# A one-core transformer block: two modulation rows change place, a reciprocal and a set of attention masks move ahead in DVE's order

## The chip, the core and the metric

The kernel runs on one core of a Trainium2 chip. A core has a matrix engine (PE), a vector engine (DVE), an activation engine (ACT), a general engine (POOL) and a queue engine (SP) that here only issues DMA transfers. Each engine runs its own instructions in the order in which they were written and waits on semaphores where an operand, or room for a result, comes from elsewhere. PE writes its products into banks of a small accumulation memory; DVE and ACT read them from there. The metric is the device time of one execution in microseconds (us).

## The reference

One decoder block on 512 tokens of width 1024, all in f32. A conditioning vector gives nine modulation vectors of 1024 (a shift, a scale and a gate for each of three sub-layers):

```
mod = silu(c) @ w_ada + b_ada
sh1, sc1, gt1, sh2, sc2, gt2, sh3, sc3, gt3 = split(mod, 9)
u = rmsnorm(h, g1) * (1 + sc1) + sh1;  h = h + 0.5 * gt1 * swiglu(u, w_ffn1_in, w_ffn1_out)
u = rmsnorm(h, g2) * (1 + sc2) + sh2;  h = h + gt2 * token_mixing(u)
u = rmsnorm(h, g3) * (1 + sc3) + sh3;  h = h + 0.5 * gt3 * swiglu(u, w_ffn2_in, w_ffn2_out)
return rmsnorm(h, g_final)
```

`swiglu` is `(silu(a) * b) @ w_out` with `a, b = split(u @ w_in)` and 2816 hidden columns. `token_mixing` projects u once, runs a causal pooling mixer and a causal dilated window attention in three head groups with rotary q and k, merges them with sigmoid gates and projects back.

## The kernel before

Activations lie with features on the 128 partitions and tokens along the row: H is eight tiles of 128 x 512. A product in f32 precision is made of three matmuls: a value is split into a high part and a rest, and `mm3` adds high times high, high times rest and rest times high. Weights come from memory in chunks of 128 x 1024 (or 768), issued by SP (L295, named after their source: `wf1i`, `wf1o`, `wmix`, `wf2i`, `wf2o`) into a few buffers, `raw` and parts of `X`. For each chunk ACT writes the high part `whi` (L377) and DVE the rest `wlo` (L389) into a ring that PE reads. A buffer is loaded again when its `wlo` has been written. Large products of the feed-forwards and the gates are made from seven block products instead of eight, with sums of blocks made by DVE (`duo`, `out_blocks`).

The order on each engine is the order in which the program calls its helpers; there is no planner. Work that is not tied to a place is put in by hand.

Such work are the modulation rows. Each of the 72 rows is 128 values of `mod`: SP loads a 128 x 1024 piece of `w_ada` (L440), and DVE multiplies it with the conditioning and sums along the row (`ada_do`, L448). `bg()` does the next row and then starts the load of a later one into a free buffer; `ada_stop` says up to which row. After every eighth row two small operations finish the vector (L459, L461). Rows 24 to 39 belong to gate, shift and scale around the first feed-forward's end, and are done within its hidden pairs: `ROWS` says after which of a pair's seven block products a row stands. Rows from 40 on are done in the mixer.

The first feed-forward's output comes in five parts over the hidden columns. The last part (columns 16 to 21, `ffn` at its end and `out_tail`) goes tile by tile. Tiles 0 to 3 are done whole: PE makes the product, DVE adds it to H (L1272), ACT squares H, DVE adds the square to AR, which collects the sum for the next norm (L499). Tiles 4 to 7 are done in two halves of 256 tokens: first half of all four, then second half of all four (L582, L583, L623). While PE is at the second halves, the first half's norm is finished: PE sums AR over the partitions (`stats_t`, L509), ACT takes the root, DVE the reciprocal `r` (L514), PE spreads it (`spread`, L519), and `norm_steps` makes the normalised halves, per tile one scaled `ev` (L533), the high part UH by ACT (L545) and the rest UL by DVE (L559).

`head` then starts the next sub-layer, the mixer or the second feed-forward, with four weight chunks at once. It runs the first half's eight feature tiles, puts the second half's statistics in after four steps, spreads them after eight, and goes on with the second half. Its ACT table changes there, from the root to what the sub-layer needs.

In the mixer's first stretch, v of the first head group is projected in four token blocks (the loop with `rope_b`), then q and k of the other groups tile by tile with attention steps hooked in at the sixth of eight feature steps: scores on PE, masks and row maxima on DVE (`at_exp`, L1472), exponentials on ACT, and one tile later the transposes on PE (`at_turn`, L1489).

## Time and profile before

| what | value |
|---|---|
| median of three executions | 970.0 us (968.23 to 970.03) |
| the profiled execution | 969.99 us, span 968.2 us |
| PE busy | 958.5 us, 99% of the span |
| DVE busy | 840.3 us, 87% |
| ACT busy | 539.3 us, 56% |
| POOL busy | 89.8 us, 9% |
| DMA issues of modulation rows on SP | 512 KB each, landing after 3.5 to 8.8 us, median 5.1 |

The span is what the profile covers; the execution's own time is 1.8 us more. A row of a timeline has the start, the busy time, the engine, the line and the operation with its output and inputs; in brackets stands how long the engine was idle before it and what ended that. Busy times of neighbours overlap a little, those of matmuls by more than half, so the time that one costs is the distance between two starts. A DVE operation on 128 x 1024 values takes 1.2 us of busy time, a matmul on 256 tokens follows the last after 0.11, one on 512 after 0.23.

### The profile page before, as it was taken

To read this page: it belongs to the slowest core of one execution; us is meant where nothing else is said; L and a number is where in the kernel's file an instruction comes from. 1 tells how busy PE (TensorE), PEld (TensorE's weight loads), DVE (VectorE), ACT (ScalarE), POOL (GpSimd) and SP (SyncE) were. 2 spreads that over 40 slices of the span, in tenths; PEclk is the share of its full clock that TensorE was granted. 3 is DMA by queue.
4 is the path that set the end of the run, shared out by engine and by line. 5 is a ranking of instruction groups with operands and counts; after the bars stand their busy time and mean duration, and the time that the engine had idled before them with its cause. 6 is when DMAs were issued, how large, how long until landed. Compare 5 with 4: busy or idle time off the path is not lost.

```text
span 968.2 us, 18169 instructions
## 1 busy us (share of the span) xinstructions
PE 958.5 (99%) x7296; PEld 899.9 (93%) x7296; DVE 840.3 (87%) x1237; ACT 539.3 (56%) x813; POOL 89.8 (9%) x106
## 2 busy tenths in 40 slices
PE   9999999999999999999999999999999999999997
PEld 7888999999999899778889998998999999999997
DVE  7989999899998778787897877989799888989886
ACT  5443666665755553444565453365666747566655
POOL 0000110101010003005510000000101000110002
PEclk9999999999999999999999999999999999999999
DMA  9857785776768648766457445723757666665632
GB/s 353 283 178 257 197 239 156 202 212 153 219 176 246 171 148 238 239 206 188 90 141 199 124 126 207 243 73 104 194 141 198 170 157 167 172 171 143 169 83 88
DMA packets 54087, 174.71 MB, mean 180 GB/s; under 512 B 7793, under 2 KB 10481, under 8 KB 53746
## 3 DMA queue, kind: packets, MB, share of 16 engines
q1 hardware_dynamic: 44416, 141.29, 44.2%
q0 software_dynamic: 9008, 31.72, 18.1%
q8 instruction: 57, 0.93, 0.4%
q10 hardware_dynamic: 578, 0.53, 0.2%
q14 instruction: 28, 0.23, 0.1%
HBM read 135.36 MB, written 2.24 MB: 142 GB/s over the span
## 4 chain that ended last, share of the span: by engine, by line
PE 84%; DVE 7%; DMA 4%; issue 2%; ACT 1%; POOL 0%; SPq 0%; POOLq 0%; DVEq 0%; ACTq 0%
PE bank L750 13%; PE bank L749 12%; PE bank L751 12%; PE bank L421 7%; PE bank L422 7%; PE bank L423 7%; PE bank L1109 4%; PE bank L1108 4%; PE bank L1110 4%; DVE wlo L389 2%; PE bank L2119 2%; PE bank L2121 1%; PE bank L2123 1%; DMA v<-wada 1%; DMA cs<-wada 1%
## 5 line engine op out<-in xcount | busy, mean ns | idle before, releaser
L389 DVE TENSOR_TENSOR wlo<-raw,whi 128x1024 fp32r<-128x1024 f32 (+3 forms) x150 | 166.4, 1118 | 37.7 <-ACT whi L377 37.5
L749 PE MATMUL bank<-UH,whi 128*128 128x256 f32 x672 | 185.7, 276 | 0.0
L750 PE MATMUL bank<-UL,whi 128*128 128x256 f32 x672 | 185.6, 276 | 0.0
L751 PE MATMUL bank<-UH,wlo 128*128 128x256 f32 x672 | 185.6, 276 | 0.0
L389 DVE TENSOR_TENSOR wlo<-X,whi 128x1024 fp32r<-128x1024 f32 (+3 forms) x133 | 142.2, 1082 | 17.8 <-ACT whi L377 17.6
L377 ACT ACTIVATE whi<-raw 128x1024 fp32r<-128x1024 f32 (+3 forms) x150 | 142.6, 964 | 22.1 <-DMA raw<-wf1o 8.4
L377 ACT ACTIVATE whi<-X 128x1024 fp32r<-128x1024 f32 (+3 forms) x133 | 123.0, 946 | 51.0 <-DVE X L312 46.1
L750 PEld LDWEIGHTS bank<-UL,whi 128*128 128x128 f32 x672 | 126.3, 188 | 0.0
L749 PEld LDWEIGHTS bank<-UH,whi 128*128 128x128 f32 x672 | 126.1, 188 | 0.2
L751 PEld LDWEIGHTS bank<-UH,wlo 128*128 128x128 f32 x672 | 126.2, 188 | 0.0
L751 PE MATMUL bank<-SH,wlo 128*128 128x256 f32 x408 | 112.7, 276 | 0.2 <-DVE wlo L389 0.2
L749 PE MATMUL bank<-SH,whi 128*128 128x256 f32 x408 | 112.6, 276 | 0.0
L750 PE MATMUL bank<-SL,whi 128*128 128x256 f32 x408 | 112.6, 276 | 0.0
L421 PE MATMUL bank<-UH,whi 128*128 128x512 f32 (+1 forms) x272 | 93.0, 342 | 0.0
L422 PE MATMUL bank<-UL,whi 128*128 128x512 f32 (+1 forms) x272 | 92.0, 338 | 0.0
L423 PE MATMUL bank<-UH,wlo 128*128 128x512 f32 (+1 forms) x272 | 91.8, 337 | 0.0
L751 PEld LDWEIGHTS bank<-SH,wlo 128*128 128x128 f32 x408 | 76.6, 188 | 0.4 <-DVE wlo L389 0.4
L749 PEld LDWEIGHTS bank<-SH,whi 128*128 128x128 f32 x408 | 76.6, 188 | 0.0
L750 PEld LDWEIGHTS bank<-SL,whi 128*128 128x128 f32 x408 | 76.6, 188 | 0.0
L1108 PE MATMUL bank<-HI,whi 128*128 128x256 f32 x224 | 61.8, 276 | 0.0
L1109 PE MATMUL bank<-HK,whi 128*128 128x256 f32 x224 | 61.8, 276 | 0.0
L1110 PE MATMUL bank<-HI,wlo 128*128 128x256 f32 x224 | 61.8, 276 | 0.0
(406 smaller groups left out, 2410.9 us busy)
## 6 DMA issues: line engine op xcount, KB each, us to landing
raw<-wmix SPq DMA_DIRECT2D x44, 512.0 KB, 4.3
raw<-wf1i SPq DMA_DIRECT2D x32, 512.0 KB, 5.9
raw<-wf2i SPq DMA_DIRECT2D x30, 512.0 KB, 4.3
ada<-wada SPq DMA_DIRECT2D x23, 512.0 KB, 5.2
X<-raw POOLq DMA_DIRECT2D x23, 512.0 KB, 6.0
xs<-wada SPq DMA_DIRECT2D x17, 512.0 KB, 5.3
X<-wf2i SPq DMA_DIRECT2D x14, 512.0 KB, 4.5
X<-wf1i SPq DMA_DIRECT2D x11, 512.0 KB, 4.6
```

The source lines that it names most:

```text
L377: self.nc.scalar.activation(self.hi[:, y], r[:, x], AF.Copy)
L389: self.nc.vector.tensor_tensor(self.lo[:, y], r[:, x], self.hi[:, y], op=OP.subtract)
L421: M(ps, hi, uh, start=start, stop=False)
L422: M(ps, hi, ul, start=False, stop=False)
L423: M(ps, lo, uh, start=False, stop=stop)
L749: M(o, hi, uh, start=start and p == 0 and k == 0, stop=False, skip_group_check=True)
L750: M(o, hi, ul, start=False, stop=False, skip_group_check=True)
L751: M(o, lo, uh, start=False, stop=k == 3, skip_group_check=True)
L1108: M(o, hi, uh, start=start and m % 2 == 0 and k == 0, stop=False, skip_group_check=True)
L1109: M(o, hi, ul, start=False, stop=False, skip_group_check=True)
L1110: M(o, lo, uh, start=False, stop=k == 1, skip_group_check=True)
L2119: M(b, hi, self.UH[k], start=k == 0, stop=False)
```

## The change

Four places in the program change.

The hidden pair at column 20 keeps one row in `ROWS` and loses two, rows 38 and 39. They are done in the last output part: `give` hands a part of `X` to the rows when the last output weights in it are split, row 38 stands at the end of tile 3, row 39 in `out_tail` behind the first half of tile 4.

In `head`, at the fifth step, the second half's statistics, root, reciprocal and table load are issued ahead of that step's normalisation, and the normalisation runs one tile less ahead. Both calls of `head` are changed by it.

In the mixer, the last token block of v does one row instead of two, and the first q tile one more, behind the masks of the first attention step.

```diff
-ROWS = {6: (6,), 8: (1, 3, 6), 12: (3, 6), 16: (3, 6), 18: (0, 1, 3, 4, 6), 20: (0, 2, 3)}
+ROWS = {6: (6,), 8: (1, 3, 6), 12: (3, 6), 16: (3, 6), 18: (0, 1, 3, 4, 6), 20: (0,)}
...
-    def out_tail(self, ms, ksrc, gate, nxt, squares):
+    def out_tail(self, ms, ksrc, gate, nxt, squares, beside=None):
...
                 self.split_lo()
                 self.fetch()
+                if beside and h == 0 and m == ms[0]:
+                    beside()
...
                 if h == 0:
-                    stepA(min(i, 5) + 3)
                     if i == 4:
                         self.stats_t(self.spare()[1], Bh)
                         nc.scalar.preload_act_table(table)
+                    stepA(min(i, 5) + 2)
                     if i == 8:
                         self.spread(self.spare()[1], Bh)
...
                 if m:
                     self.split(self.done)
                 self.fetch()
-            self.out_tail((4, 5, 6, 7), ks, gate, 1, lambda m: self.X[0][:, m % 2 * HT:])
+                self.give()
+                if m == 3:
+                    self.bg()
+            self.out_tail((4, 5, 6, 7), ks, gate, 1, lambda m: self.X[0][:, m % 2 * HT:], self.bg)
+            assert self.ada_next == 40 and not self.adat, self.ada_next
+            self.ada_free = None
+
+    def give(self):
+
+        for x in list(self.retired):
+            if not any(x is b for b in self.buf.values()):
+                self.retired = [y for y in self.retired if y is not x]
+                self.ada_free.append(x)
+        self.bg_fetch()
...
-            self.ada_free, self.ada_stop = [self.cs, self.AR], 40
+            self.ada_free, self.ada_stop = [self.cs, self.AR], 38
...
-            assert self.ada_next == 40 and not self.adat, self.ada_next
-            self.ada_free = None
+            assert self.ada_next == 38 and not self.adat, self.ada_next
+            self.ada_free, self.ada_stop = [], 40
...
-                for _ in range((0, 0, 1, 2)[n]):
+                for _ in range((0, 0, 1, 1)[n]):
...
-                        more = [(2, self.bg)] if dst is self.qt[1] and hp else []
+                        more = [((2, 7)[not hp], self.bg)] if dst is self.qt[1] else []
```

The order on DVE at the last hidden pair, before; `cs` and `AR` with `cond` are the rows 38 and 39, `wide` the hidden values, `HK` their rest:

```order
L781 TENSOR_TENSOR HK<-wide,HI 128x1024
L448 SCALAR_TENSOR_TENSOR cs,mod<-cs,cond 128x1024
L389 TENSOR_TENSOR wlo<-X,whi 128x1024
L389 TENSOR_TENSOR wlo<-raw_64,whi 128x768
L448 SCALAR_TENSOR_TENSOR AR,mod<-AR,cond 128x1024
L459 TENSOR_TENSOR mod<-mod,vecs 128x8
L461 SCALAR_TENSOR_TENSOR mod<-mod,vecs 128x8
L389 TENSOR_TENSOR wlo<-X,whi 128x768
```

and with the change:

```order
L783 TENSOR_TENSOR HK<-wide,HI 128x1024
L389 TENSOR_TENSOR wlo<-X,whi 128x1024
L389 TENSOR_TENSOR wlo<-raw_64,whi 128x768
L389 TENSOR_TENSOR wlo<-X,whi 128x768
L389 TENSOR_TENSOR wlo<-raw_65,whi 128x768
L793 TENSOR_TENSOR wide<-ev 128x2x256
L389 TENSOR_TENSOR wlo<-raw_63,whi 128x768
L821 TENSOR_TENSOR wide<-ev,bank_91 128x2x256
L776 TENSOR_TENSOR wide<-wide 128x1024
```

Four of the eight operations are gone from here; the weight splits and the last pair's own operations close up.

The order on DVE where tile 3 ends and the halves of tiles 4 and 5 begin, before; the first row is H of tile 3, the first of 256 columns that of tile 4:

```order
L1272 SCALAR_TENSOR_TENSOR H<-bank_90,mod,H 128x512
L389 TENSOR_TENSOR wlo<-raw_64,whi 128x1024
L499 TENSOR_TENSOR AR<-AR,ev 128x512
L582 SCALAR_TENSOR_TENSOR H<-bank_91,mod,H 128x256
L389 TENSOR_TENSOR wlo<-raw_65,whi 128x1024
L623 TENSOR_TENSOR AR<-AR,X 128x256
L582 SCALAR_TENSOR_TENSOR H<-bank_96,mod,H 128x256
```

and with the change, where `X` with `cond` are the two rows:

```order
L1274 SCALAR_TENSOR_TENSOR H<-bank_90,mod,H 128x512
L389 TENSOR_TENSOR wlo<-raw_64,whi 128x1024
L499 TENSOR_TENSOR AR<-AR,ev 128x512
L448 SCALAR_TENSOR_TENSOR X,mod<-X,cond 128x1024
L582 SCALAR_TENSOR_TENSOR H<-bank_91,mod,H 128x256
L389 TENSOR_TENSOR wlo<-raw_65,whi 128x1024
L448 SCALAR_TENSOR_TENSOR X,mod<-X,cond 128x1024
L459 TENSOR_TENSOR mod<-mod,vecs 128x8
L461 SCALAR_TENSOR_TENSOR mod<-mod,vecs 128x8
L625 TENSOR_TENSOR AR<-AR,X 128x256
L582 SCALAR_TENSOR_TENSOR H<-bank_96,mod,H 128x256
```

The same four operations now stand on both sides of the first half of tile 4.

The order on DVE ahead of the first attention step, before; `xs` with `cond` are rows, `prob` with `masks` the masks:

```order
L448 SCALAR_TENSOR_TENSOR xs,mod<-xs,cond 128x1024
L459 TENSOR_TENSOR mod<-mod,vecs 128x8
L448 SCALAR_TENSOR_TENSOR xs,mod<-xs,cond 128x1024
L389 TENSOR_TENSOR wlo<-raw_63,whi 128x1024
L1472 ISA prob,m_3527<-bank_93,masks 128x128
```

and with the change:

```order
L448 SCALAR_TENSOR_TENSOR xs,mod<-xs,cond 128x1024
L459 TENSOR_TENSOR mod<-mod,vecs 128x8
L389 TENSOR_TENSOR wlo<-raw_63,whi 128x1024
L1487 ISA prob,m_3527<-bank_93,masks 128x128
L1487 ISA m_3527 128x1
L1487 ISA prob,m_3527<-bank_94,masks 128x128
L1487 ISA m_3527 128x1
L1489 TENSOR_SCALAR negmax<-m_3527 128x2
```

The second row has left the place ahead of the masks; it stands behind both sets of them.

## The prediction

> **What bounds the kernel now.** I read the page's part 1 first, then the waits of the PE, then its timeline at each place where one matmul starts later after the last than its kind does elsewhere.
>
> ```profile
> PE 958.5 (99%) x7296; PEld 899.9 (93%) x7296; DVE 840.3 (87%) x1237; ACT 539.3 (56%) x813; POOL 89.8 (9%) x106
> ```
>
> PE, the matmul engine, is at work almost throughout. So a change that adds and removes no matmul can only gain what PE loses in short stops, and can only lose by making new ones. The stops come out of start times, since the busy times overlap. The first is at the start of the last output part of the first feed-forward (PE, timeline):
>
> ```profile
> 318.15 0.39 PE L421 MATMUL bank<-HI,whi 128*128 128x512 f32 x1
> 319.19 0.50 PE L422 MATMUL bank<-HK,whi 128*128 128x512 f32 x1 [0.65 <-DVE HK L781]
> 319.53 0.40 PE L423 MATMUL bank<-HI,wlo 128*128 128x512 f32 x1
> 319.77 0.40 PE L421 MATMUL bank<-HI,whi 128*128 128x512 f32 x1
> ```
>
> Three matmuls take 1.62 us here, where one follows another after 0.23 (319.53 and later): 0.93 lost, waiting for HK, the low half of the last hidden pair. The second kind is at the two `head`s, where PE spreads the second half's statistics (L519). The first three rows are the same spread for the first half, which waits for nothing; then the second half before the mixer, and before the second feed-forward:
>
> ```profile
> 343.10 0.28 PE L423 MATMUL bank<-HI,wlo 128*128 128x256 f32 x1
> 343.21 0.61 PE L519 MATMUL bank<-cst,r 128*128 128x128 f32 x4
> 343.58 0.37 PE L421 MATMUL bank<-HI,whi 128*128 128x256 f32 x1
> ...
> 353.24 0.28 PE L423 MATMUL bank<-UH,wlo 128*128 128x256 f32 x1
> 353.65 0.71 PE L519 MATMUL bank<-cst,r 128*128 128x128 f32 x4
> 354.11 0.36 PE L421 MATMUL bank<-UH,whi 128*128 128x256 f32 x1
> ...
> 640.39 0.28 PE L423 MATMUL bank<-UH,wlo 128*128 128x256 f32 x1
> 641.13 0.71 PE L519 MATMUL bank<-cst,r 128*128 128x128 f32 x4 [0.46 <-DVE r L514]
> 641.60 0.37 PE L421 MATMUL bank<-UH,whi 128*128 128x256 f32 x1
> ```
>
> From the matmul ahead of the spread to the one behind it: 0.48 without a wait, 0.87 and 1.21 with one. Lost: 0.39 and 0.73. The last is the first attention step, four transposes of probabilities, beside eight of the next step:
>
> ```profile
> 392.29 1.39 PE L1489 MATMUL bank<-cst,prob 128*128 128x128 f32 x4
> 393.43 0.48 PE L421 MATMUL bank<-UH,whi 128*128 128x512 f32 x1
> ...
> 406.35 1.04 PE L1489 MATMUL bank<-cst,prob 128*128 128x128 f32 x8
> 407.14 0.48 PE L421 MATMUL bank<-UH,whi 128*128 128x512 f32 x1
> ```
>
> Eight take 0.79, so four should take 0.40; these took 1.14: 0.74 lost. Together 2.79 us, and each of the four lies where the change has an edit.
>
> **The change part by part.** The sum is made against the profiled execution, 969.99 us with a span of 968.2; the median of the three runs is 970.0, the same.
>
> Rows 38 and 39 leave the last hidden pair. What DVE and ACT do there:
>
> ```profile
> 309.99 1.22 DVE L448 SCALAR_TENSOR_TENSOR AR<-AR,cond 128x1024 f32<-128x1024 f32 x1
> ...
> 311.55 0.96 DVE L389 TENSOR_TENSOR wlo<-X,whi 128x768 fp32r<-128x768 f32 x1
> ...
> 315.55 1.23 DVE L774 TENSOR_TENSOR wide<-wide 128x1024 f32<-128x1024 f32 x1
> 317.91 1.23 DVE L781 TENSOR_TENSOR HK<-wide,HI 128x1024 fp32r<-128x1024 f32 x1 [1.13 <-ACT HI L756]
> ...
> 312.89 0.60 ACT L771 ACTIVATE wide<-bank 128x512 f32<-128x512 f32 x1 [1.27 <-PE bank L751]
> 316.81 1.06 ACT L756 ACTIVATE HI<-wide 128x1024 fp32r<-128x1024 f32 x1 [3.33 <-DVE wide L774]
> ```
>
> Row 39 with its two small finishing operations takes 1.56 (309.99 to 311.55). Row 38 is the same dot without them; busy 1.22, it gives way after about 1.14, since the rows show each next start some 0.08 before a busy time ends. Without both, DVE reaches L774 by 312.85. L774 also needs the silu of L771, done at 313.49, so it starts at 313.5, 2.05 earlier. From its start to PE's on HK was 3.64 (315.55 to 319.19); PE could go on at 317.2 and wants HK at 318.38. The stop goes whole, with 1.2 in hand: **-0.93**.
>
> The rows come back in the tail of the same part, where DVE updates H (L1272, L582), ACT squares it and DVE adds the square to AR (L623). Row 38 stands ahead of the H of tile 4 (332.62), row 39 behind the weight split that follows it:
>
> ```profile
> 330.21 0.75 DVE L1272 SCALAR_TENSOR_TENSOR H<-bank,mod,H 128x512 f32<-128x512 f32 x1 [0.45 <-PE bank L423]
> ...
> 332.62 0.48 DVE L582 SCALAR_TENSOR_TENSOR H<-bank,mod,H 128x256 f32<-128x256 f32 x1
> 333.29 1.23 DVE L389 TENSOR_TENSOR wlo<-raw,whi 128x1024 fp32r<-128x1024 f32 x1 [0.19 <-ACT whi L377]
> ...
> 336.32 0.43 DVE L623 TENSOR_TENSOR AR<-AR,X 128x256 f32<-128x256 f32 x1 [0.48 <-ACT X L583]
> 336.66 0.48 DVE L582 SCALAR_TENSOR_TENSOR H<-bank,mod,H 128x256 f32<-128x256 f32 x1
> 337.69 0.42 DVE L623 TENSOR_TENSOR AR<-AR,X 128x256 f32<-128x256 f32 x1 [0.54 <-ACT X L583]
> ...
> 340.54 0.48 DVE L582 SCALAR_TENSOR_TENSOR H<-bank,mod,H 128x256 f32<-128x256 f32 x1 [0.58 <-PE bank L423]
> ...
> 342.66 0.17 DVE L514 RECIPROCAL r<-r 128x2 f32<-128x2 f32 x1 [0.68 <-ACT r L511]
> ```
>
> H of tile 3 waits for PE, so it comes 0.93 earlier, and DVE reaches the place of row 38 at 331.69. Row 38 to 332.83, H to 333.23, the split to 334.38, row 39 with its small operations to 335.94, the add of tile 4 to 336.28. From there H to H is 1.37 (1.03 for the square and back, 0.34 for the add): tiles 5, 6 and 7 bring DVE to tile 4's second half at 340.39, where PE, 0.93 ahead, offers it at 339.61. The reciprocal follows 2.12 later (340.54 to 342.66), at 342.51; PE follows a reciprocal by about 0.2 and would spread at 342.73. It wants to at 343.21 - 0.93 = 342.28. So a new stop of 0.45, and some 0.09 for starting again: **+0.5**. Behind the late DVE wait H, the normalised halves and so the `head`; they are as late as the spread and no later. Bounds: 0, if the gaps that DVE has here (0.48 and 0.54 a tile) swallow more; 2.7, if all 1.14 + 1.56 comes through.
>
> The loads of the two rows move on SP's queue, from ahead of the last six output-weight loads to between two mixer loads, of which this is the second:
>
> ```profile
> 327.78 0.33 SPq L295 DMA_DIRECT2D raw<-wmix  x1
> ...
> DMA to landing us min/median/max: 3.5/5.1/8.8
> ```
>
> The other line is for all loads of modulation weights. Both must be issued before the load that was at 327.78, thus by 326.85 at the latest; that load waits for a buffer split later than theirs, so it loses nothing. Landing after 5.1, row 39's weights are there at 331.9, and DVE wants them at 334.4. Costed at nothing; the cover is 2.4 us of landing time, and at 8.8 DVE would wait 1.2. The six output-weight loads no longer stand behind them and can only come sooner.
>
> In `head` the reciprocal steps ahead of the last first-half normalisation, and ACT's square root and table load ahead of the last UH. Second `head`:
>
> ```profile
> 640.38 0.24 ACT L511 ACTIVATE r<-bank,eps 128x2 f32<-128x2 f32 x1
> 640.64 1.28 ACT L646 ACT_TABLE_LOAD   x1
> ...
> 640.91 0.16 DVE L514 RECIPROCAL r<-r 128x2 f32<-128x2 f32 x1
> ...
> 642.94 0.49 DVE L559 SCALAR_TENSOR_TENSOR UL<-ev,mod,UH 128x256 fp32r<-128x256 f32 x1 [0.18 <-ACT UH L545]
> ```
>
> One step is two DVE operations of 0.4, so the root moves from 640.38 to 639.6 and the reciprocal from 640.91 to about 639.9: ahead of 640.39, where PE asks. **-0.73**, and likewise **-0.39** before the mixer. What is late instead: the last UH, now behind the table load, to 641.5, and the first second-half result, from 643.4 to about 643.5. PE has 48 matmuls at 0.11, 5.5 us, between spread and second half; starting 0.73 earlier it comes there at 646.4. Covered by 2.9; without that cover it is a wait of the same length as the lateness.
>
> The Trainium skill ("ScalarE: Activation LUTs", section "Table sets: the hidden batching unit") speaks against this step: it prices a change of table set at about 2.7 us. This trace has 1.28, which decides. By the page, an estimate, the second head's results would come 1.4 later, the weight split behind them would hold PE up to 0.8, and the sum would be near 968.5; that belongs to the second rival below.
>
> In the attention one row moves behind the first masks:
>
> ```profile
> 388.61 1.23 DVE L448 SCALAR_TENSOR_TENSOR xs<-xs,cond 128x1024 f32<-128x1024 f32 x1 [1.08 <-DMA xs<-wada]
> ...
> 390.90 0.28 DVE L1472 CUSTOM_DVE_ANT_0 prob<-bank,masks 128x128 f32<-128x128 f32 x1
> ```
>
> That row waited 1.08 for its load and took 1.14 with the masks queued behind it. They start 2.2 earlier, at 388.7, and what was done at 393.43 could be at 391.2; PE, 0.8 ahead by then, asks at 391.5. **-0.74**. The row runs later, in time that DVE has gained.
>
> Sum: -0.93 + 0.5 - 0.39 - 0.73 - 0.74 = -2.3, so **967.7 us**.
>
> **The rivals.**
> - The tail takes back what HK gave. For it: DVE there is one serial chain with ACT, and the rows carry 2.7 us. Against: DVE also has gaps and starts 0.93 early. The tail's cost is then 1.6 to 2.7: 968.8 to 969.9, about 969.2.
> - The swap in `head` only moves the wait: DVE stands at the reciprocal and what is normalised behind it holds PE instead. For it: DVE would indeed wait some 0.4 there. Against: the 2.9 of cover. Without 0.39 and 0.73: 968.8.
> - The gaps absorb both rows, the tail costs nothing: 967.2.
> - Slower: the rows' loads land late, since mixer loads share the DMA engines, and DVE stands in the serial tail with PE behind it. It decides from a landing at 334.4, and each us after is a us lost. To be slower by 1.94 it must eat 2.29 + 1.94 = 4.2 beyond the 0.5: a landing 11.8 us after 326.85, where the longest seen is 8.8. At 4.5 beyond: 972.2.
>
> **How the numbers follow.** 0.2%, about what a measurement of this kernel tells from no change, is 1.94 us, so faster means under 968.06. Chances: the forecast 0.50, the tail 0.22, the swap 0.12, the absorbed rows 0.12, slower 0.04. The forecast's own range is 966.9 to 968.5, by the tail's cost; about 0.43 of its 0.50 is under 968.06, and with the absorbed rows faster is 0.55, slower 0.04, the rest 0.41. The range goes up into the tail's case, 969.8, and down to 966.1, since one of the three runs before was 1.8 under the other two.
>
> **What would show it.** Right: no wait of L422 for HK; 0.48 round the L519 of the second half in both heads; four transposes in 0.4; a stop of about 0.45 at the first-half L519 in the tail. Wrong: a stop at that L519 above 1 us or one at L509 ahead of it (the tail's case), a DVE wait for X<-wada (late loads), or new stops where PE enters the second half of a `head`.

## The result, and the profile after

| | before | changed |
|---|---|---|
| median, executions side by side on one chip | 970.0 us (968.01 to 970.84, 9) | 967.13 us (966.24 to 968.6, 9) |
| ratio of the two, with its 95% interval | | 0.9975 (0.9965 to 0.9985) |
| the profiled execution | 969.99 us, span 968.2 | 966.33 us, span 964.5 |

The changed kernel is faster by 2.9 us in the medians and by 2.4 by the ratio, and the forecast was 967.7. On another chip the same two gave 968.96 (29 executions) and 966.97 (12), 2.0 apart, with a ratio of 0.9981 (0.9968 to 0.9993), which is 1.8. So the change is worth some 2 to 3 us, with the forecast's 2.3 between. The two profiled spans differ by 3.7, and that is more than the change: part of it, below, is that two executions of one program differ.

First the list of what PE waited for, in the changed kernel (waits for, in all, how many, the longest):

```profile
PE bank L2035 <- DVE ones L2040: 1.1, 1, 1.1
PE bank L2134 <- ACT UH L545: 0.5, 1, 0.5
PE bank L509 <- ACT ev L930: 0.2, 1, 0.2
```

The two first rows are the start of the program, the third its end; the kernel before has them too. These three of its list are gone, and so is one of 0.4 at its start:

```profile
PE bank L422 <- DVE HK L781: 0.6, 1, 0.6
PE bank L519 <- DVE r L514: 0.5, 1, 0.5
PE bank L751 <- DVE wlo L389: 0.2, 1, 0.2
```

The list is of idle time behind the busy time of a matmul, and a stop that is little longer than that busy time is not in it: neither the 0.39 at the mixer's `head` before nor the tail's new stop, so the starts have to be read as well. Now the four places of the forecast in the changed kernel's timelines; its lines lie up to 15 below those of before (L774 is L776 there, L781 is L783, L623 is L625, L1489 is L1504). DVE at the last hidden pair, at rows 38 and 39 in their new place, in the tail and in the second `head`:

```profile
313.00 1.23 DVE L776 TENSOR_TENSOR wide<-wide 128x1024 f32<-128x1024 f32 x1 [0.18 <-ACT wide L773]
315.36 1.23 DVE L783 TENSOR_TENSOR HK<-wide,HI 128x1024 fp32r<-128x1024 f32 x1 [1.13 <-ACT HI L758]
...
331.12 1.22 DVE L448 SCALAR_TENSOR_TENSOR X<-X,cond 128x1024 f32<-128x1024 f32 x1
...
333.80 1.22 DVE L448 SCALAR_TENSOR_TENSOR X<-X,cond 128x1024 f32<-128x1024 f32 x1
...
341.83 0.17 DVE L514 RECIPROCAL r<-r 128x2 f32<-128x2 f32 x1 [0.67 <-ACT r L511]
...
636.47 0.17 DVE L514 RECIPROCAL r<-r 128x2 f32<-128x2 f32 x1 [0.33 <-ACT r L511]
```

PE at HK, at the tail's spread, at the second-half spread of both `head`s, and at the first attention step:

```profile
317.64 0.39 PE L421 MATMUL bank<-HI,whi 128*128 128x512 f32 x1
317.87 0.39 PE L422 MATMUL bank<-HK,whi 128*128 128x512 f32 x1
...
341.69 0.28 PE L423 MATMUL bank<-HI,wlo 128*128 128x256 f32 x1
342.05 0.71 PE L519 MATMUL bank<-cst,r 128*128 128x128 f32 x4
342.52 0.37 PE L421 MATMUL bank<-HI,whi 128*128 128x256 f32 x1
...
352.18 0.28 PE L423 MATMUL bank<-UH,wlo 128*128 128x256 f32 x1
352.30 0.61 PE L519 MATMUL bank<-cst,r 128*128 128x128 f32 x4
352.66 0.37 PE L421 MATMUL bank<-UH,whi 128*128 128x256 f32 x1
...
636.99 0.28 PE L423 MATMUL bank<-UH,wlo 128*128 128x256 f32 x1
637.10 0.61 PE L519 MATMUL bank<-cst,r 128*128 128x128 f32 x4
637.47 0.37 PE L421 MATMUL bank<-UH,whi 128*128 128x256 f32 x1
...
389.82 0.60 PE L1504 MATMUL bank<-cst,prob 128*128 128x128 f32 x4
390.17 0.48 PE L421 MATMUL bank<-UH,whi 128*128 128x512 f32 x1
```

HK is read 0.23 after the matmul before it, so there is no stop. Both heads go over the spread in 0.48, and the four transposes take 0.35. The tail has the one new stop at a spread: 0.83 from 341.69 to 342.52, where 0.48 is undisturbed, so 0.35.

PE issues the same 7296 matmuls in the same order in both kernels, so the start of each can be compared, and what a stretch takes more than in the best profile of that stretch is what it lost. This table, worked out so from the start times, holds all profiles of this study. The columns are places on the clock of the kernel before; "behind" is what the matmuls up to the next column lost by a longer step from one to the next, of which more below.

```
lost, us              row 36  HK    tail  behind mixer behind 2nd   behind 1st    2nd
                      at 304  319   343   343    head  354    head  641    attn.  attn. step
before                0.47    0.93  -     -      0.40  1.04   0.73  -      0.78   -
before, again         0.73    0.93  -     -      0.39  -      0.72  -      0.31   -
changed               -       -     0.34  0.01   -     -      -     -      -      -
changed, again        -       -     0.36  0.30   -     -      -     -      -      -
rows only             0.78    -     0.34  0.30   -     -      0.72  -      0.70   -
swap only             0.45    0.92  -     -      -     -      -     -      1.40   -
masks only            -       0.83  -     -      0.40  0.01   0.62  0.63   -      0.71
rows left out         0.55    -     -     -      -     -      -     -      -      -
DVE held in heads     -       -     0.35  -      0.89  0.01   1.33  -      -      0.07
rows sooner           1.19    -     -     -      -     -      -     -      -      -
both                  -       -     -     -      -     -      -     -      -      1.88
both, again           -       -     -     -      -     -      -     -      -      -
row behind copies     -       -     -     -      -     -      -     -      -      0.33
```

The first 16 us differ by up to 0.5 from one execution to the next and are not in it, nor are 0 to 0.5 at 628 and, in "rows left out", 0.25 of longer steps behind the stop at 304. It also leaves out 0.09 at L509, just ahead of the tail's spread: this stands in the four profiles that have the 0.34 to 0.36 beside it, and in no other, so it belongs to the tail's price.

In the rows of the two first profiles, before and changed, the terms that were forecast give 0.93 + 0.40 + 0.73 + 0.78 - 0.34 - 0.09 = 2.4. Another 1.5 in that table was not forecast: 0.47 at 304, where nothing is changed, and 1.04 between 354 and 382. PE's last matmul starts 4.1 earlier in all; the two programs' ends behind it differ by 0.4, which leaves the 3.7 of the spans. For the 1.04, this is one stretch of 12 us in both, as PE's busy time, the matmuls that fall into it, the granted clock, the DMA share and the GB/s that DMA moved; the kernel before, then the changed one:

```profile
354.20:366.20 12.00, 12.00 (x104) 1.00 0.71 250
```

```profile
354.20:366.20 12.00, 12.00 (x108) 1.00 0.70 227
```

PE waits for nothing and has its full clock in both, and the transfers have about the same share; yet 104 matmuls fall into the one and 108 into the other. The starts show two regular steps for a matmul of 256 columns: 114, 113, 113 ns, again and again, in the changed kernel (mean 113.3), and 117 to 119 ns (mean 117.8) in the kernel before, for 249 matmuls.

### The profile page after: what moved, and what is told of

Read it like the earlier page. It is cut to its first block, busy times and chain, and to the rows that moved or that the text cites. A ratio compares the mean times of both kernels' runs of the same rounds, so it can differ in the third digit from the quotient of the medians.

```text
span 964.5 us, 18166 instructions
## 1 busy us (share of the span) xinstructions
PE 956.2 (99%) x7296; PEld 898.9 (93%) x7296; DVE 839.8 (87%) x1237; ACT 539.5 (56%) x813; POOL 89.8 (9%) x106
## 4 chain that ended last, share of the span: by engine, by line
PE 97%; issue 1%; DMA 1%; POOL 0%; ACT 0%; DVE 0%; SPq 0%; POOLq 0%
PE bank L753 14%; PE bank L752 14%; PE bank L751 14%; PE bank L421 9%; PE bank L422 9%; PE bank L423 9%; PE bank L1112 5%; PE bank L1111 5%; PE bank L1110 5%; PE bank L2134 2%; PE bank L2136 2%; PE bank L2138 2%; PE bank L1471 1%; PE bank L1780 1%; PE bank L1522 1%; PE bank L1781 1%
```

## The experiments

### The change in its three parts

**Rows only.** The changed kernel with the old order in `head` and at the masks:

```
+                    stepA(min(i, 5) + 3)
                     if i == 4:
...
-                    stepA(min(i, 5) + 2)
...
-                for _ in range((0, 0, 1, 1)[n]):
+                for _ in range((0, 0, 1, 2)[n]):
...
-                        more = [((2, 7)[not hp], self.bg)] if dst is self.qt[1] else []
+                        more = [(2, self.bg)] if dst is self.qt[1] and hp else []
```

> Only rows 38 and 39 are moved; the two heads and the order of attention masks and row are as in the kernel before. The forecast's own terms: no stop of PE at L422 for HK (-0.93), a stop of about 0.4 at the first-half L519 in the tail (+0.5 forecast, +0.43 seen with the whole change), and still there: the stops at the second-half L519 (0.39 and 0.73) and the 0.74 at the transposes L1489. Rival, the tail takes back what HK gave: then the tail loses 0.9 or more. On the 256-column matmuls behind the mixer's second-half L519, which followed each other after 117.8 ns until 382 in the kernel before and after 113.3 ns in the changed one (1.0 in all): theory A, the stop at that L519 leaves PE in the slower pace, expects 117.8 here too, since the stop is here; theory B, the moved rows (what DVE and the transfers do beside those matmuls) made it, expects 113.3.

Measured, one execution: 969.48 us, beside 969.01 for one of the kernel before. HK's stop is gone and the tail has 0.34; the second head's 0.72 and 0.70 at the transposes stay, as expected. So the tail takes back less than half of what HK gave (0.34 at the spread and 0.09 ahead of it, of 0.93), and the rival that it takes back all falls. Unexpected: the mixer head's stop is gone without the swap. Behind the tail's stopped spread PE's step was 117.8 ns, which lost 0.30 up to 353; with the 0.34 ahead of it PE came to the head later by more than the 0.40 of that stop, and the reciprocal was there. Behind that head the steps were 113.3. That is the number of theory B, but the case that A speaks of, a stop there, did not occur; and what the tail shows, the longer step from a stop to the next spread without one, is A's mechanism in a place that it had not named.

**Swap only.** The kernel before with only `stepA` and the statistics exchanged:

```
-                    stepA(min(i, 5) + 3)
                     if i == 4:
                         self.stats_t(self.spare()[1], Bh)
                         nc.scalar.preload_act_table(table)
+                    stepA(min(i, 5) + 2)
```

> Only the order in the two heads is changed (reciprocal and square root ahead of the last first-half normalisation); rows 38, 39 and masks as in the kernel before. The forecast's terms: -0.39 at the mixer's second-half L519 and -0.73 at the second feed-forward's; HK's stop of 0.93 and the 0.74 at the transposes stay; no new stop where PE enters the second half. Rival, the swap only moves the wait: new stops of 0.4 to 0.7 at the first matmuls of the second half. Pace behind the mixer's second-half L519: theory A (the stop leaves PE in the slower pace) expects 113.3 ns until 382, thus another -1.0 in this kernel; theory B (the moved rows made it) expects 117.8 as before.

Measured, one execution: 968.53 us. Both stops at the heads are gone (0.40 and 0.73), HK's 0.92 stays, no new stop stands at the entry to a second half, and the steps behind both heads are 113.3, without the rows' move, as A expects and B does not. The rival that the swap only moves the wait falls. The transposes lost 1.40 here, where the kernel before lost 0.78. PE comes to them 1.27 earlier than in the first profile of the kernel before, but the load of the row ahead of the masks lands only 0.65 earlier (387.94 against 388.59): what PE gains ahead of this place it loses again here in part, as long as the masks wait for that load.

**Masks only.** The kernel before with the two lines on the rows:

```
-                for _ in range((0, 0, 1, 2)[n]):
+                for _ in range((0, 0, 1, 1)[n]):
...
-                        more = [(2, self.bg)] if dst is self.qt[1] and hp else []
+                        more = [((2, 7)[not hp], self.bg)] if dst is self.qt[1] else []
```

> Only the row of the first attention step is moved behind its masks; the rest as in the kernel before. The forecast's term: four transposes in 0.4 in place of 1.14 (-0.74), nothing else. Rival, the row then makes PE wait later in the attention: a new stop up to 1.1 where the masks of the next step are needed. Pace behind the mixer's second-half L519: theory A expects 117.8 ns (the stop of 0.39 is there), theory B 117.8 as well; a third, that the pace differs from one execution to the next of the same program, allows either.

Measured, one execution: 969.32 us. The transposes lose nothing; but 0.71 comes back one step later. PE at the second attention step, of this kernel and of the changed one:

```profile
403.98 0.40 PE L423 MATMUL bank<-UH,wlo 128*128 128x512 f32 x1
404.22 1.74 PE L1489 MATMUL bank<-cst,prob 128*128 128x128 f32 x8
405.72 0.48 PE L421 MATMUL bank<-UH,whi 128*128 128x512 f32 x1
```

```profile
402.85 0.39 PE L423 MATMUL bank<-UH,wlo 128*128 128x512 f32 x1
403.08 1.04 PE L1504 MATMUL bank<-cst,prob 128*128 128x128 f32 x8
403.88 0.48 PE L421 MATMUL bank<-UH,whi 128*128 128x512 f32 x1
```

Eight transposes take 1.50 from the first to what follows, not 0.80. The rival that the change makes a later wait in the attention was right, though not by its mechanism: DVE does not wait for the moved row's load but for `rt<-tr`, four copies of 64 KB that turn q for the rotary factors. DVE in "masks only":

```profile
397.71 0.69 DVE L1419 TENSOR_TENSOR rt<-rt,cs 128x512 f32<-128x512 f32 x1 [3.43 <-DMA rt<-tr]
```

The next masks stand behind this. The copies stand behind the 512 KB load of a row on SP's queue; that load lands at 396.84, the copies from 397.02 to 397.58. And behind the second head's stop of 0.62 the steps were 117.8 until 658 (0.63 lost), while behind the mixer head's they were 113.3: the other way round than in the first profile of the kernel before. So A falls in its plain form, since this stop at the mixer's spread was followed by 113.3, and B as well, which had expected 117.8 there; the third, that it differs from one execution to the next, is left.

### The tail by itself

**Rows left out.** The changed kernel without rows 38 and 39:

```
-                if m == 3:
-                    self.bg()
-            self.out_tail((4, 5, 6, 7), ks, gate, 1, lambda m: self.X[0][:, m % 2 * HT:], self.bg)
+            self.out_tail((4, 5, 6, 7), ks, gate, 1, lambda m: self.X[0][:, m % 2 * HT:])
...
+            self.ada_next = self.ada_ahead = 40
+            self.nc.vector.memset(self.mod[:, 38:40], 0.0)
+            self.ada_fin("scale", 32, 40, self.g(1))
```

> The changed kernel with rows 38 and 39 of the modulation left out (their loads and their dots; two of the eight tiles of that scale vector are zero). It measures the tail's term by itself: by the forecast the stop at the first-half L519 in the tail (0.43 with the rows) is gone, and PE's last instruction comes 0.4 earlier than in the changed kernel. Rival, the stop is not of the rows but of PE coming 0.93 earlier to a chain of DVE and ACT that is no faster: then a stop of 0.2 to 0.4 stays at that L519 without the rows. Pace behind the mixer's second-half L519: theory A expects 113.3 ns, theory B may give either.

Measured, one execution: 967.21 us. The tail's stop is gone altogether, so it was the rows', and the rival (PE merely arrives earlier) falls. That PE's last instruction would come earlier failed: it came 0.7 later than in the changed kernel's first profile, since this execution lost 0.55 + 0.25 at and behind 304 and 0.4 at the start. A single time does not show 0.4 us here; the place in the trace does.

**Rows sooner.** Row 38 at the end of tile 2, row 39 at the end of tile 3, none in the tail:

```
-                if m == 3:
+                if m > 1:
                     self.bg()
-            self.out_tail((4, 5, 6, 7), ks, gate, 1, lambda m: self.X[0][:, m % 2 * HT:], self.bg)
+            self.out_tail((4, 5, 6, 7), ks, gate, 1, lambda m: self.X[0][:, m % 2 * HT:])
```

> The changed kernel with row 38 at the end of tile 2 of the last output part and row 39 at the end of tile 3, both ahead of the tail (in the changed kernel: end of tile 3, and first step of the tail). Row 38 then stands in the 0.45 for which DVE waits ahead of the H of tile 3. My theory (the tail's stop is DVE's lateness by the two rows): the stop of 0.35 at the first-half L519 goes or falls below 0.1, and with no stopped L519 left none is followed by 117.8 ns: 0.4 to 0.6 us faster than the changed kernel, 966.6 in the mean. Rival: the serial chain of H, square and add sets it and the rows' place does not matter: the stop stays at 0.3 or more. Second rival: row 38's load has not landed there, DVE waits for X<-wada and the tail's stop grows.

Measured: 967.1 us (965.75 to 967.68, 10 executions), ratio to before 0.998 (0.997 to 0.9989). PE in the tail:

```profile
342.80 0.28 PE L423 MATMUL bank<-HI,wlo 128*128 128x256 f32 x1
342.92 0.61 PE L519 MATMUL bank<-cst,r 128*128 128x128 f32 x4
343.28 0.37 PE L421 MATMUL bank<-HI,whi 128*128 128x256 f32 x1
```

0.48 again: the stop is gone with both rows done, by the order alone, and neither row waited for its load. Both rivals fall. The 0.4 to 0.6 that I expected in the time did not come: the mean is 967.0, not 966.6, and the median is 967.1 against 967.13 of the changed kernel on another chip. The profiled execution lost 1.19 at 304.

### The longer step

**The kernel before, again.**

> The kernel before, unchanged, profiled once more. Terms that are of the program must come again: HK's stop 0.8 to 0.95, the stops of 0.39 and 0.73 at the second-half L519, 0.74 at the transposes. Terms that I hold for differences from one execution to the next may not: the stop at 304 (0 to 0.5, by when the load of row 36 lands), the stop ahead of L509 at 628 (0 to 0.45). Pace of the 256-column matmuls: of seven L519 in front of which PE had stopped, three were followed by 117.8 ns and four by 113.3; of those without a stop none. Theory C (a stop there leaves PE in one of two paces, and which one turns on a few ns) expects either of the two behind each stopped L519; theory A (a stop always slows) expects 117.8 behind both stops; rival D, that the program alone decides, expects exactly the paces of the first profile: 117.8 behind the mixer's, 113.3 behind the second feed-forward's.

Measured: 968.69 us, beside a median of 968.84 (16 executions) of the same program. HK, 0.39 and 0.72 are there to 0.01. At 304 it lost 0.73, not 0.47, and at the transposes 0.31, not 0.78: that term turns on when a load lands. And behind the mixer's stopped spread the steps were 113.3. The same program gave 117.8 in one execution and 113.3 in another, so rival D falls, and with it 1.04 of the first comparison as something that the program decides.

**DVE held in the heads.** The changed kernel with three operations of 128 x 512 on DVE ahead of each second-half reciprocal:

```
+                        z = self.R[:, :T]
+
+                        def hold():
+                            for _ in range(3):
+                                nc.vector.tensor_tensor(z, z, z, op=OP.max)
-                        self.stats_t(self.spare()[1], Bh)
+                        self.stats_t(self.spare()[1], Bh, between=hold if n else None)
```

> The changed kernel with DVE held up in both heads, by three operations of 128x512 each (they write what they read) ahead of the second-half reciprocal, so that PE stops again at the second-half L519: by some 0.3 to 0.6 before the mixer and likewise before the second feed-forward, and 0.35 at the first-half L519 in the tail as in the changed kernel. Theory C expects each of the three stopped L519 to be followed by 113.3 or 117.8 ns, and never anything between, until matmuls of another width; theory A expects 117.8 behind each stop that is longer than 0.3. If the rows or transfers set the pace (theory B), it stays at 113.3 in all three, as in the profile of the changed kernel. Whole: the changed kernel + 0.8 to 1.5, and + 1.0 for each that goes slow.

Measured, one execution: 968.62 us. The stops were 0.89 and 1.33, longer than I expected, and 0.35 in the tail. Behind all three the steps were 113.3, so theory A falls here too: a stop need not bring the longer step. C allows it, but three times the same shows nothing by itself.

**The changed kernel, again.** This ran beside the two kernels of the next part.

> The changed kernel, unaltered, beside the two that follow. By the stops seen so far its time is 966.2 where nothing is late, and more by what differs from one execution to the next: 0.3 to 0.8 at 304 (load of row 36), 0.4 where the tail's stopped L519 leaves the slower pace, 0.6 to 1.8 at the second attention step (406 on the clock of the kernel before), where the copies rt<-tr land late: so between 966.0 and 968.7, median about 967. If these stops are not what makes its executions differ, the two kernels below spread as widely as this one.

Measured: 966.97 us (966.2 to 969.93, 12 executions), three of them from 968.9 to 969.9, above the range that I gave; none of the three was profiled, so what held them stays open. The stretch behind the tail's spread, in this profile and then in the first one of the same program:

```profile
343.20:352.20 9.00, 9.00 (x79) 1.00 0.35 107
```

```profile
343.20:352.20 9.00, 9.00 (x82) 1.00 0.37 109
```

Equal clock, 3 matmuls of 82 fewer, and no more DMA beside them (107 GB/s with the longer step, 109 without; in the first comparison 250 with it, 227 without). The gap ahead of this spread was 385 ns in the one and 359 in the other.

Over the 13 profiles there are 39 spreads L519 in the tail and the two heads. Ahead of each stand the small matmuls of the statistics, L509, and from them to the spread the step is 117.8 in 38 of the 39, with no stop. Behind the 26 spreads in front of which PE had not stopped the step was 113.3 each time: there the spread ends the longer step. Of the 13 with a stop, nine were followed by 113.3 and four by 117.8, and there was nothing between the two steps. In three of these four the longer step stood ahead of the spread already and went on; in the fourth, in the tail of "changed, again", 113.3 stood ahead of it and 117.8 behind, so there the stopped spread began it. The gaps ahead of the four were 355, 385, 410 and 635 ns; with 359, 362, 406, 412, 734, 735 and 739, among others, the step was 113.3. So either step can stand behind a stop, as theory C has it, and the length of the stop does not tell which, since 410 lies between 406 and 412; that it turns on a few ns is not shown.

Nor is L509 a sure switch: ahead of the two other spreads, at 629 and 950, the step was 117.8 in one and in ten of the 13 profiles. Other places have the longer step too: 39 matmuls ahead of the second head in two profiles, the 68 behind the stop at 304 in "rows left out", and in all 13 profiles 23 matmuls at 484 and 70 at 502. What PE or its memory does differently in the longer step stays open.

### Row 36, and the copies of the second attention step

**Both.** Rows 38 and 39 sooner, and row 36 behind L821 and L776, row 37 behind HK:

```
-ROWS = {6: (6,), 8: (1, 3, 6), 12: (3, 6), 16: (3, 6), 18: (0, 1, 3, 4, 6), 20: (0,)}
+ROWS = {6: (6,), 8: (1, 3, 6), 12: (3, 6), 16: (3, 6), 18: (0, 1, 3, 4), 20: (0, 2)}
```

> As the kernel with rows 38 and 39 sooner, and rows 36 and 37 later: row 36, whose load DVE waits 1.9 to 2.8 us for with L821 and L776 queued behind it, stands behind these two, and row 37 behind HK. Theory: the stop of 0.3 to 0.5 at L751 to L753 (304), which four of six profiles show, is DVE's wait for that load, so it goes in all executions: 0.2 to 0.4 faster in the mean than with rows 38 and 39 sooner alone. Rival: row 37 behind HK delays the splits there and the last hidden pair, and HK or a weight split holds PE at 305 to 319 by up to 1.1: slower by that.

Measured: 966.26 us (966.17 to 968.3, 7 executions), ratio to before 0.9973 (0.9962 to 0.9984). The rows' order in the tail is that of "rows sooner". The stop at 304 is gone and nothing was held behind row 37. But the execution that was profiled is the one of 968.3, and it lost 1.88 at the second attention step, by the wait that "masks only" had shown:

```profile
397.50 0.69 DVE L1434 TENSOR_TENSOR rt<-rt,cs 128x512 f32<-128x512 f32 x1 [3.48 <-DMA rt<-tr]
```

Here the load ahead of the copies is not all of it: that lands at 394.92 and the first two copies at 395.26 and 395.65, but the other two only at 397.06 and 397.38.

**Both, again.**

> The kernel with rows 38 and 39 sooner and rows 36 and 37 later, once more. Of its seven executions six were within 966.17 to 966.57; the seventh, 968.3, was the profiled one and had a stop of 1.8 at the second attention step. Theory: of the three causes of differences only that one is left in this kernel, so its times are again near 966.3 but for one in four to one in eight at 967 to 968.3. Rival: 966.3 was chance, and its times spread from 966 to 968 as the changed kernel's do.

Measured: 966.49 us (965.54 to 967.07, 12 executions), ratio to before 0.9971 (0.9961 to 0.9981). Its profile has no loss at any of the places of the table. The slower ones that I expected did not come: none of 12 was above 967.1. Beside it, on the same chip, three of 12 of the changed kernel were at 968.9 and more. Row 36 still waits for its load, but with nothing behind it that PE needs soon; DVE in this profile:

```profile
296.81 0.68 DVE L821 TENSOR_TENSOR wide<-ev,bank 128x512 f32<-128x512 f32 x1
297.59 1.23 DVE L776 TENSOR_TENSOR wide<-wide 128x1024 f32<-128x1024 f32 x1
299.97 1.23 DVE L448 SCALAR_TENSOR_TENSOR cs<-cs,cond 128x1024 f32<-128x1024 f32 x1 [1.15 <-DMA cs<-wada]
```

With the old order of rows 36 and 37, six of ten profiles lost 0.45 to 1.19 at 304; with the new one none of three. This kernel is the best of the study by its median, 0.48 under the changed one, though the intervals of the two ratios overlap.

**Row behind copies.** The kernel "both" with the moved row one tile later, and its load on SP's queue behind the copies:

```
-                        more = [((2, 7)[not hp], self.bg)] if dst is self.qt[1] else []
+                        more = [(2, self.bg), (3, self.bg)] if dst is self.qt[1] and hp else []
```

> The kernel before this one, with the row that the change moved behind the first attention step's masks put one tile later, into the time in which DVE waits for the copies rt<-tr; with it goes its load, from just ahead of those copies on SP's queue to behind them. Theory (the copies land late because a load of 512 KB that the moved row set free stands right ahead of them): median landing of rt<-tr falls from 3.5 to 5.8 us (six profiles with the masks moved) towards the 2.3 of the kernel before, DVE's wait at L1434 falls under 2, no stop at the second attention step, and all executions within 966.0 to 966.7. Rival: the copies are late from the two loads that stay ahead of them or from others in flight; then 3.5 and more again, and the slow executions of 967 to 968.3 stay. Second rival, slower: the row's load, issued 3.5 later, lands after DVE wants it, a wait for xs<-wada of up to 2 holds the masks or L1434.

Measured: 966.58 us (966.09 to 967.93, 12 executions), ratio to before 0.9976 (0.9966 to 0.9986). The issue groups of "both" and then of this kernel, size and median time to landing:

```profile
rt<-tr SPq DMA_DIRECT2D x4, 64.0 KB, 5.2
```

```profile
rt<-tr SPq DMA_DIRECT2D x4, 64.0 KB, 2.9
```

The copies land after 2.3, 2.3, 2.3 and 2.6 in the four profiles with the masks' old order, after 3.5 to 5.8 in the eight with the new one, and after 2.9 here. So the load ahead of them on the queue makes them late: in the seven of the eight profiles that show its landing, the first copy lands 0.17 to 0.33 us behind it. The Trainium skill ("DMA: Bandwidth & Descriptors", section "Queues, rings and completion order") says that each DMA engine takes the entries of one ring in order; these landings agree.

That load stands there in all eight, though, and only two of them lost more than 0.07 at the second attention step. What sets these two apart is not shown, but the traces have one candidate. In each a single transfer of 16 KB on the queue that the DMA view calls `instruction` falls into this stretch. In the six it starts 1.0 to 1.2 us after the issue of the load, in "masks only" 1.8 after and in "both" 4.8 after, ahead of the two copies that land last.

With the load behind the copies the gain went elsewhere, as the second rival said. DVE here:

```profile
393.39 0.69 DVE L1434 TENSOR_TENSOR rt<-rt,cs 128x512 f32<-128x512 f32 x1 [0.37 <-DMA rt<-tr]
...
396.98 1.23 DVE L448 SCALAR_TENSOR_TENSOR xs<-xs,cond 128x1024 f32<-128x1024 f32 x1 [2.17 <-DMA xs<-wada]
```

The wait at L1434 fell to 0.37, and a row's load, issued behind the copies here, holds DVE for 2.17 with the same masks behind it: 0.33 lost at the second attention step, and times no narrower than before.

## Why the prediction was right, point by point

- **HK, -0.93: right.** L776 was forecast for 313.5 and came at 313.00, on a clock 0.51 earlier (PE's matmul ahead of HK starts at 317.64 where before it was 318.15, mainly since nothing was lost at 304): the same to 0.01. PE took HK at 317.87, 2.51 after L783 began, where the kernel before needed 1.28 from one to the other: 1.23 in hand, forecast 1.2. The stop was 0.83 to 0.93 in the four profiles that kept rows 38 and 39 and 0 in all that moved them.
- **The tail, +0.5: right.** 0.34 to 0.36 at the spread in all four profiles where the rows stand there, and 0.09 at L509 ahead of it: 0.44. A stop at L509 had been named as a sign of the tail's case, but this one is far from the 1.6 to 2.7 of that rival. The reciprocal was forecast for 342.51 and came at 341.83 + 0.51 = 342.34; DVE was 0.06 earlier at row 38 (331.12 + 0.51 against 331.69) and gained another 0.11 by the tail's end. "Rows left out" and "rows sooner" bring it to 0. What the forecast did not have is that this stop, like those of the heads, can leave PE at the longer step: 0.30 in two of the four.
- **The loads of rows 38 and 39, nothing: right.** Neither row waits for `X<-wada` in the changed kernel; row 39's weights land at 327.57 and DVE comes to them at 333.80. So the slower rival with its landing after 11.8 us has nothing to stand on.
- **The two heads, -0.39 and -0.73: right.** "Swap only" shows them alone. (In "rows only" the mixer's stop went without the swap, so in the whole change the -0.39 is not the swap's alone.) The second head's reciprocal was forecast for 639.9 on the clock of before. In the changed kernel PE's spread is at 637.10 where before it could have been at 640.50, 3.40 more, so its reciprocal at 636.47 stands for 639.87. Nothing is lost where PE enters a second half, so the cover of 2.9 held and the rival "the swap only moves the wait" fell. ACT's table load in its new place, in the changed kernel:

```profile
636.46 1.28 ACT L647 ACT_TABLE_LOAD   x1
```

  The Trainium skill ("ScalarE: Activation LUTs", section "Table sets: the hidden batching unit") puts a change of table set at about 2.7 us. Here the load takes 1.28, as before, and ACT's next operation starts at 637.75, 0.01 behind it; this does not agree, and the measurement decides.
- **The first attention step, -0.74: right in the one execution it was read from, but not the whole price.** The term is the landing of one load, the row's ahead of the masks, against PE's coming: 0.78, 0.31, 0.70 and 1.40 in four profiles with the old order, 0.80 in the mean. From that landing to the time at which PE could start the transposes there were 3.70, 4.18, 3.79 and 3.08 us, and with the loss that makes 4.48 or 4.49 each time. And the step failed in "The row runs later, in time that DVE has gained": with it, copies of 64 KB come to stand directly behind a load of 512 KB, and two of the eight profiles with this order lost 0.71 and 1.88 one attention step later, and a third 0.07: 0.33 in the mean of the eight. The net is near -0.5, an estimate from these profiles.
- **What was left out.** That the stops at the spreads cost more than themselves: a stopped spread left the step at 117.8 ns in 4 of 13, and 0.30 to 1.04 more was lost behind it. The change takes away two stopped spreads and makes one. By the mean of the profiles with a stop this is worth -0.26 behind the mixer's head (1.04 in one of four), -0.13 behind the second (0.63 in one of five) and +0.15 in the tail (0.30 in two of four): -0.24, an estimate from few cases.

With these the sum is -0.93 + 0.44 - 0.40 - 0.73 - 0.50 - 0.24 = -2.36, an estimate, where the forecast had -2.3 and the two chips measured -2.0 and -2.9. That the totals agree so well is partly luck: the forecast's term for the attention was too large by some 0.24, and the longer step, worth as much in the same direction, was missing. The rival that the gaps absorb both rows named 967.2, which is nearer to the measured 967.1 than the forecast, but its mechanism is not there: the tail's stop is. The median of 970.0 that it started from was also high for this program, which gave 968.8 and 969.0 elsewhere.

## What to carry to other kernels

On an engine that never idles, price each short stop by the distance between starts, and follow each moved instruction on its own engine and on the queue whose loads it releases: a transfer that is let go sooner can stand in front of a small one that somebody waits for. Where a term rests on when one load lands, take it from several profiles, since one shows a single draw of it. And before explaining a difference between two traces, profile the same program twice: here 1.5 of the 4.1 us between the two timelines of PE belonged to the execution, not to the change.

## What the runs showed of the hardware that was not expected

- PE has two steps for the same matmul of 256 columns, 113.3 and 117.8 ns, at a granted clock of 1.00 and with no wait. It changes over at small matmuls of 128 columns or at stops, not alike in two executions of one program: in the tail and the heads the longer step follows L509 in 38 of 39 cases (at two other places in 11 of 26), the shorter one follows a spread without a stop in 26 of 26 and a spread after a stop in 9 of 13. The longer step can last: 249 matmuls and 28 us in one case. By the Trainium skill ("TensorE: Matmul & The Clock Gate", section "Wait — 56ns, not 53.3ns?"), 256 columns would take 109.2 ns at full clock, an estimate from its formula; neither step is that, and the measurement decides. No run here shows what makes the two.
- A load of 512 KB in front of four copies of 64 KB on one queue made their median time to landing 3.5 to 5.8 us, where it was 2.3 to 2.6 without it.
- The landing of row 36's load decided up to 0.78 us at 304, in a stretch that the change does not touch; the 1.19 of "rows sooner" has a wait of 0.33 for row 37's load in it.
